# Weight sums of a seven-product matrix multiplication moved to accumulating DMAs in DRAM, with two of the seven split weights stored ahead and loaded as they are

## The chip, the cores and the metric

One NeuronCore of a Trainium2 chip runs one program. The metric is device microseconds (us) of one execution; less is better. Three runs of the kernel before took 936.91, 937.03 and 938.17 us, so its median is 937.03 us. Engines are named as the profile names them: PE (TensorE matmul; PEld its weight loads), DVE (VectorE), ACT (ScalarE), POOL (GpSimd) and SP (SyncE, which here only issues DMAs).

## What is computed

A decoder trunk of two layers on 512 tokens of width 1024, all float32: an mLSTM layer, then a gated linear attention (GLA) layer, each inside RMS norms with a residual. The change lies in the GLA layer, mostly in its last product:

```python
def gla_mixer(h, w_in, w_gate_up, b_gate, norm_w, w_out):
    p = jnp.einsum('btd,de->bte', _f32(h), _f32(w_in))      # q, k, v, z, r are slices of p
    ...
    o = gla_chunked(q * (G_KEY_HEAD ** -0.5), k, v, log_a)   # 4 heads, values 4 x 512
    on = o * lax.rsqrt(jnp.mean(o * o, axis=-1, keepdims=True) + NORM_EPS)
    y = on.reshape(B, T, D_INNER) * _f32(norm_w) * jax.nn.silu(z)
    return jnp.einsum('bte,ed->btd', y, _f32(w_out))         # (512 x 2048) by (2048 x 1024)
# in reference():  x = x + rms_norm(out, post_norm_w[i])
```

## The kernel before

**Split products.** PE multiplies in a reduced float format (fp32r). To keep float32 accuracy every operand is split in two: `hi` is the operand rounded (a CAST on ACT, line 137) and `lo` the remainder (a subtraction on DVE, line 138). Each product is three matmuls: hi by hi, hi by lo, lo by hi. Weights come from DRAM in chunks of 128 x 1024 (512 KB). A chunk is loaded into one of three `raw` buffers (SP, line 154) and split into one of four pairs of buffers `whi`, `wlo`; PE reads those. So a split of chunk number j+4 waits until PE is done with chunk j.

**Order.** PE, ACT and DVE run in the order in which the Python code emits the work. `run_jobs` goes through a list of jobs; ahead of each job it emits the splits of chunks up to `LA` = 3 chunks further on, then what earlier jobs deferred with `later(k, ...)` (k jobs later), then one item or more of `steps` and `spare`, and then the job itself. SP and POOL are ordered by the scheduler of the framework; each of them, too, works strictly in its order.

**The end of the GLA layer**, in the order of PE: for heads 0 to 3, v products (`gv`, 4 chunks a head), attention (`o`) and z products (`gz`, 4 chunks a head) alternate; the last of them is the attention of head 3, `g_att(3)`. Then comes the product by `w_out`. It is cut 2 x 2 x 2 and done with seven half-size products (Strassen-Winograd) instead of eight: P1 to P7, each of 4 chunks; a chunk meets 2 blocks of tokens, 12 matmuls in all. The seven need sums of the quarters A11, A12, A21, A22 of the weights: U = A21 + A22 for P5, U - A11 for P6, A12 - (U - A11) for P3, A22 - (U - A11) for P7. POOL forms them in SBUF, chunk by chunk (lines 1241, 1246, 1257, 1263). The other side needs sums of quarters of y: `combine` (lines 1200 to 1202), and one subtraction in `g_y` (line 1135), on POOL and DVE. Products go to PSUM in the order P1 and P5 in turn, P2 and P3 in turn, P6, the rest of P3, P7, P4. Each half row of the result is summed, squared for the norm (ACT, line 1304), multiplied by the norm's weights `pw` (POOL, line 1310; DVE for the last two), scaled and added to the residual `xr` (DVE, line 1326), and stored (SP, line 1327). The residual itself, `x1_d`, was written to DRAM at the start of the layer.

```python
        return source([(w_gout[1, 0, c], lambda: t5("sm")[:, 0:1024]), (w_gout[1, 1, c], None)], form=f,
                      after=to_s2, free=(1, 0))          # P5: loads A21 and A22, POOL adds them
    ...
    SRC = {"P1": p1, "P5": p5, "P2": p2, "P7": p7, "P3": lambda c: source([], form=lambda: raw12[c]),
           "P6": lambda c: source([], form=lambda: sm[c], free=(0, 0))}
```

Of the kernel before, what the change touches and what calls it, by code (L numbers as in the profile page):

```python
# [95 lines left out]
def tile_mlstm_gla(ctx, tc, xT, pvec, cst, wg, wgv, w_min, w_qk, w_v, w_mout,  # L96
# [8 lines left out]
    ctx.enter_context(tc.manual_schedule(engines={mybir.EngineType.PE, mybir.EngineType.Activation,  # L105
                                                  mybir.EngineType.DVE}))

# [949 lines left out]
    def full_qk(w, j, after):  # L1057
        def run(chunk):
            ev = gqk(w, j, chunk)
            later(1, lambda: (ev(), after and after()))  # L1060

        job(run, ring(w_gqk[w, j]))
# [16 lines left out]
    def gv_job(h, c):  # L1079
        def run(chunk):  # L1080
            if c == 0:
                st["gv", h] = [psum("gv") for _ in range(4)]
            pss = st["gv", h]
            natural(pss, chunk, 2 * c, ghi2, glo2, 8)
            if c == 3:
                def evac():
                    VS[h] = t2s("gvhi", 4, F32R), t2s("gvlo", 4, F32R)
                    for i in range(4):
                        hi, lo = VS[h][0][i], VS[h][1][i]
                        nc.scalar.activation(hi, pss[i], AF.Identity, scale=rcol[:, i:i + 1])  # L1090
# [5 lines left out]
        job(run, ring(w_gv[h, c]))  # L1096

# [31 lines left out]
    def g_y(h, vt):  # L1129
# [9 lines left out]
    def gz_job(n):  # L1139
        def run(chunk):  # L1140
# [10 lines left out]

        job(run, ring(w_gz[n]))

    job(lambda: nc.vector.reduce_max(mx, nref, axis=AX.X), n=0)
    gz_job(0)
# [9 lines left out]
    for h in range(NH):  # L1165
        if h + 1 < NH:
            for c in range(4):
                gv_job(h + 1, c)
        if h == NH - 1:
            job(lambda: [operand("2", k, Y[1, k]) for k in range(4)], n=0)  # L1170
            job(lambda: [combine(k, nc.gpsimd) for k in range(4)], n=0)
        job(lambda h=h: g_att(h))
        if h + 1 < NH:
            gz_job(4 * h + 4)
            job(lambda h=h: (g_rstd(h), split_scores(h + 1)), n=0)
            for i in range(1, 4):
                gz_job(4 * h + 4 + i)
# [17 lines left out]

    def combine(k, eng):

        y1, y2 = Y[0, k], Y[1, k]
        a, b = HALF
        eng.tensor_sub(y1[:, b], y2[:, b], y1[:, b])  # L1200
        eng.tensor_sub(y1[:, a], y1[:, b], y1[:, a])  # L1201
        eng.tensor_sub(y2[:, a], y2[:, a], y1[:, b])

# [5 lines left out]
    def block(name, k):  # L1209
        what, half = {"P1": ("1", 0), "P5": ("1", 1), "P2": ("2", 0), "P3": ("2", 1),  # L1210
                      "P7": ("3", 0), "P6": ("3", 1), "P4": ("4", k % 2)}[name]
        return [z[:, HALF[half]] for z in OPS[what, k // 2 if what == "4" else k]]

    bank, sums, parts = {}, {}, {}

    def product(name, to, chunks, tb, c0=0):
# [3 lines left out]
        for c, (whi, wlo) in enumerate(chunks):  # L1220
            for i in range(2):
# [8 lines left out]
    sm, raw11, raw12, raw22, last = ([None] * 4 for _ in range(5))  # L1230
    sub = nc.gpsimd.tensor_sub

    def p1(c):
        def f(a11):
            raw11[c] = a11
            return a11
        return source([(w_gout[0, 0, c], lambda: t5("a11")[:, 0:1024])], form=f, free=(0, 0))

    def p5(c):
        def f(a21, a22):  # L1240
            nc.gpsimd.tensor_add(a21, a21, a22)
            sm[c] = a21
            return a21

        def to_s2():
            sub(sm[c], sm[c], raw11[c])

        return source([(w_gout[1, 0, c], lambda: t5("sm")[:, 0:1024]), (w_gout[1, 1, c], None)], form=f,
                      after=to_s2, free=(1, 0))

    def p2(c):
        def f(a12):
            raw12[c] = a12
            return a12

        def to_s4():
            sub(raw12[c], raw12[c], sm[c])

        return source([(w_gout[0, 1, c], None)], form=f, after=to_s4, free=(0, 0))

    def p7(c):
        def f(a22):
            sub(sm[c], a22, sm[c])  # L1263
            raw22[c] = a22
            return sm[c]

        def to_p4():
            last[c] = split_chunk(raw22[c], "t2")

        return source([(w_gout[1, 1, c], None)], form=f, after=to_p4)  # L1270

    SRC = {"P1": p1, "P5": p5, "P2": p2, "P7": p7, "P3": lambda c: source([], form=lambda: raw12[c]),
           "P6": lambda c: source([], form=lambda: sm[c], free=(0, 0))}
    TO = {"P1": "a", "P6": "a", "P7": "a", "P4": "a", "P5": "c", "P3": "c", "P2": "d"}

    def prod_job(name, c, n=1, la=LA):
        def run(chunk):
            for tb in range(2):
                product(name, TO[name], [chunk], tb, c)
            if c == 3:  # L1280
                if name in ("P1", "P5", "P6", "P7"):
                    AFTER[name]()
                else:
                    later(8 if name == "P2" else 2, AFTER[name])

        job(run, SRC[name](c), n=n, la=la)

# [29 lines left out]

    def row_done(r):
# [13 lines left out]
    def after_p7():  # L1332
        for tb in range(2):
            out_part(2 + tb, 1, "a", "e5", tb)
        row_done(2)
        row_done(3)

    def after_p3():
        for tb in range(2):
            out_part(2 + tb, 0, "c", "u2", tb)  # L1340

    AFTER = {"P1": lambda: keep_copy("e1", "a"), "P5": lambda: keep_copy("e5", "c"), "P6": after_p6,
             "P2": lambda: [out_part(tb, 0, "d", "e1", tb) for tb in range(2)], "P7": after_p7, "P3": after_p3}

# [6 lines left out]
    for c in range(4):  # L1351
        prod_job("P1", c)
        prod_job("P5", c)
        if c == 1:
            job(lambda: (g_rstd(NH - 1), steps.extend(
                [lambda: tail_y(0), lambda: tail_y(2), lambda: None, lambda: None]
                + [lambda k=k: (combine(k, nc.vector), combine(k + 1, nc.vector)) for k in (4, 6)]
                + [lambda k=k: (operand("3", k, Y[0, k]), operand("3", k + 1, Y[0, k + 1])) for k in range(0, 8, 2)]
                + [lambda c=c: operand4(c) for c in range(4)])), n=0)

    def load_pw():
        st["pw"] = t5("pw")[:, 0:D]
# [97 lines left out]
```

## Time and profile before

| | |
|---|---|
| median of three runs | 937.03 us |
| the profiled execution: its time | 936.81 us |
| its span, first to last instruction | 935.1 us (1.7 us lie around it) |
| PE busy | 907.2 us, 97% of the span |
| DVE, ACT, POOL busy | 653.5, 523.2, 224.3 us |
[...]
| DMA, mean over the span | 117 GB/s |

The page cuts the span into 40 slices; the engines' digits there are tenths of busy time. A "wait" row says which instruction idled and what released it. The chain of waits follows the work that ended last back through what released it. A matmul's own duration in the records is longer than the step from one matmul to the next, since they are pipelined; the pace of PE is read from starts.

### The profile page before, as it was taken

The page shows a single profiled execution, that of the slowest core. Times are in us where ns is not written, and L with a number is a line of the kernel's source. Part 1 is how long each engine was busy: PE and PEld are TensorE (multiplying, and loading weights), DVE is VectorE, ACT ScalarE, POOL GpSimd, SP SyncE. Part 2 cuts the span into 40 slices and gives each one's busy share as a digit, 9 for nine tenths or more (in the row PEclk, how much of TensorE's full clock was granted, in tenths as well). Part 3 has the DMA queues.
Part 4 walks back from the last instruction along what each step waited for, and adds up shares of the span by engine and source line. Part 5 has one row for each costly group of instructions (what it writes and reads, how often), then busy time and mean ns, then how long its engine had stood idle before and what let it go on. Part 6 is the DMA issues. An engine that isn't in the chain of part 4 may idle for free. (4 is left out here: it accounts for less than half of the span.)

```text
span 935.1 us, 12315 instructions
## 1 busy us (share of the span) xinstructions
PE 907.2 (97%) x4624; PEld 761.7 (81%) x4624; DVE 653.5 (70%) x886; ACT 523.2 (56%) x876; POOL 224.3 (24%) x152
## 2 busy tenths in 40 slices
PE   9999999999999999999999999999999999978886
PEld 7887878878877888899999987778888888866665
DVE  5999897787795678787678666632445454598986
ACT  6856676655745657685666554553334342535653
POOL 0022563154230045332001100000001011275443
PEclk9999999999999999999999999999999999998999
DMA  8334353442431312323776322222222243230232
GB/s 308 123 108 146 113 174 119 146 137 97 151 113 46 121 64 86 124 103 115 222 229 226 131 73 85 68 68 94 90 67 91 68 158 113 91 112 23 68 123 102
DMA packets 40514, 109.82 MB, mean 117 GB/s; under 512 B 4416, under 2 KB 8896, under 8 KB 40448
## 3 DMA queue, kind: packets, MB, share of 16 engines
q1 hardware_dynamic: 40160, 108.75, 35.2%
q8 instruction: 38, 0.62, 0.3%
q10 hardware_dynamic: 288, 0.22, 0.1%
q14 instruction: 28, 0.23, 0.1%
HBM read 100.56 MB, written 8.39 MB: 117 GB/s over the span
## 5 line engine op out<-in xcount | busy, mean ns | idle before, releaser
L138 DVE TENSOR_TENSOR wlo<-raw,whi 128x1024 fp32r<-128x1024 f32 (+1 forms) x138 | 180.4, 1313 | 117.5 <-ACT whi L137 116.1
L137 ACT CAST whi<-raw 128x1024 fp32r<-128x1024 f32 (+1 forms) x138 | 142.6, 1038 | 96.4 <-PE gv L122 37.7
L381 POOL TENSOR_TENSOR vp<-V,wv 128x512 f32<-128x512 f32 x56 | 88.8, 1609 | 177.4 <-ACT V L469 109.5
L122 PE MATMUL op<-yhi,whi 128*128 128x256 f32 x256 | 73.4, 287 | 0.0
L122 PE MATMUL op<-yhi,wlo 128*128 128x256 f32 x256 | 72.5, 283 | 0.4 <-DVE wlo L138 0.4
L122 PE MATMUL op<-ylo,whi 128*128 128x256 f32 x256 | 72.8, 284 | 0.0
L384 DVE SCALAR_TENSOR_TENSOR vp<-V,wv 128x512 f32<-128x512 f32 x72 | 68.0, 987 | 0.0
L122 PE MATMUL gz<-g2h,whi 128*128 128x512 f32 x128 | 51.5, 403 | 0.4 <-PEq L1113 0.4
L122 PEld LDWEIGHTS op<-ylo,whi 128*128 128x128 f32 x256 | 49.1, 192 | 1.1 <-DVE ylo L138 0.6
L122 PE MATMUL gz<-g2h,wlo 128*128 128x512 f32 x128 | 49.9, 390 | 0.0
L122 PE MATMUL gz<-g2l,whi 128*128 128x512 f32 x128 | 49.8, 389 | 0.0
L122 PE MATMUL qk<-chi,whi 128*128 128x512 f32 x128 | 49.8, 389 | 0.0
L122 PE MATMUL qk<-chi,wlo 128*128 128x512 f32 x128 | 49.8, 389 | 0.0
L122 PE MATMUL qk<-clo,whi 128*128 128x512 f32 x128 | 49.8, 389 | 0.0
L122 PE MATMUL gv<-whi,g2h 128*128 128x512 f32 x128 | 49.8, 389 | 0.0
L122 PE MATMUL gv<-wlo,g2h 128*128 128x512 f32 x128 | 49.8, 389 | 0.0
L122 PE MATMUL gv<-whi,g2l 128*128 128x512 f32 x128 | 49.8, 389 | 0.0
L122 PEld LDWEIGHTS op<-yhi,wlo 128*128 128x128 f32 x256 | 49.1, 192 | 0.6 <-DVE wlo L138 0.6
L122 PEld LDWEIGHTS op<-yhi,whi 128*128 128x128 f32 x256 | 49.1, 192 | 0.5 <-issue 0.5
L122 PE MATMUL op<-whi,yhi 128*128 128x512 f32 x96 | 38.7, 403 | 8.9 <-ACT whi L137 8.9
L122 PE MATMUL op<-wlo,yhi 128*128 128x512 f32 x96 | 39.0, 406 | 8.6 <-DVE wlo L138 8.6
L686 POOL TENSOR_TENSOR sq<-sq 128x512 f32<-128x512 f32 x12 | 17.6, 1471 | 114.2 <-ACT sq L684 95.4
(283 smaller groups left out, 2582.0 us busy)
## 6 DMA issues: line engine op xcount, KB each, us to landing
raw<-in_w_min SPq DMA_DIRECT2D x30, 512.0 KB, 3.7
raw<-in_w_mout SPq DMA_DIRECT2D x29, 512.0 KB, 4.0
wv<-in_wgv SPq DMA_DIRECT2D x32, 256.0 KB, 3.6
raw<-in_w_qk SPq DMA_DIRECT2D x16, 512.0 KB, 3.6
raw<-in_w_gqk SPq DMA_DIRECT2D x16, 512.0 KB, 4.0
raw<-in_w_gz SPq DMA_DIRECT2D x16, 512.0 KB, 3.4
raw<-in_w_gv SPq DMA_DIRECT2D x16, 512.0 KB, 3.5
raw<-in_w_gout SPq DMA_DIRECT2D x12, 512.0 KB, 3.5
```

The costliest lines, as they stand in the source:

```text
L122: nc.tensor.matmul(out, lhsT=lhsT, rhs=rhs, start=start, stop=stop, skip_group_check=more)
L137: nc.scalar.copy(hi, src)
L138: nc.vector.tensor_sub(lo, src, hi.bitcast(F32))
L381: nc.gpsimd.tensor_mul(j, V[h][i], w)
L384: nc.vector.scalar_tensor_tensor(j, V[h][i], 1.0, w, op0=ALU.mult, op1=ALU.mult, accum_out=o)
L686: nc.gpsimd.tensor_add(sqs[0], sqs[0], sqs[vt])
```

## The change

Four parts.

1. **Sums in DRAM.** The four kinds of sums (U, W, Z, R; 4 chunks each) become DRAM tensors. Signs are moved to the other side, so that only additions are left: U = A21 + A22, W = A11 + U, Z = A12 + W, R = A11 + A21. The weights in `w_gout` are unchanged; parts of y and the second half of `pw` change sign instead. Each sum is a copy (DRAM to DRAM) and then an accumulating DMA on it, 32 DMAs of 512 KB, issued by POOL beside the q and k products of the GLA layer. POOL does no arithmetic on weights any more.
2. **P3 and P7 split ahead.** Eight extra jobs (`pre_job`) between the z and v jobs load a chunk of Z or R, split it (ACT, DVE) and store both halves to DRAM (SP, four stores). At P3 and P7 POOL's DMAs load the halves straight into `whi` and `wlo`.
3. **y side and results on DVE.** `combine` for all eight k, the subtraction in `g_y` and the multiplications by `pw` move from POOL to DVE. For token rows 2 and 3 the scaled result is added to `x1_d` by an accumulating DMA (POOL) and `x1_d` is copied to the output (SP, DRAM to DRAM); rows 0 and 1 are as before.
4. **Order.** One more chunk of look-ahead at `g_att(3)` and at the jobs beside the extra ones; P4's chunks become jobs of their own, loaded again from `w_gout`; deferred steps are spaced differently; POOL's order is now the code's.

```diff
-HLA = 3
+HLA = 6
+PRE = ("P3", "P7")
     def split_chunk(raw, kind):
+        if kind == "pre":
+            hi = wp.tile([P, 1024], F32R, tag="whi", bufs=4, name="whi")
+            lo = wp.tile([P, 1024], F32R, tag="wlo", bufs=4, name="wlo")
+            for to, of in zip((hi, lo), raw):
+                nc.gpsimd.dma_start(to, of)
+            return [hi[:, 0:T], hi[:, T:]], [lo[:, 0:T], lo[:, T:]]
...
+    def weights(what, c):
+        return {"P1": w_gout[0, 0, c], "P2": w_gout[0, 1, c], "P4": w_gout[1, 1, c], "P5": wsum["U", c],
+                "P6": wsum["W", c], "P3": wsum["Z", c], "P7": wsum["R", c]}[what]
+    def pre_job(name, c):
+        def run(chunk):
+            for to, of in zip(wpre[name, c], chunk):
+                for i in range(2):
+                    nc.sync.dma_start(to[:, i * T:(i + 1) * T], of[i].bitcast(F32))
+        job(run, source([(weights(name, c), None)], "t2"), n=0)
+    def wsum_start(n, c):
+        nc.gpsimd.dma_start(wsum[n, c], {"U": w_gout[1, 0, c], "W": w_gout[0, 0, c], "Z": w_gout[0, 1, c],
+                                       "R": w_gout[0, 0, c]}[n])
+    def wsum_add(n, c):
+        nc.gpsimd.dma_start(wsum[n, c], {"U": w_gout[1, 1, c], "W": wsum["U", c], "Z": wsum["W", c],
+                                         "R": w_gout[1, 0, c]}[n], accum_op=ALU.add,
+                            max_dma_last_dim=4096)
...
-            nc.gpsimd.tensor_sub(y[:, HALF[1]], y[:, HALF[1]], y[:, HALF[0]])
+            nc.vector.tensor_sub(y[:, HALF[1]], y[:, HALF[0]], y[:, HALF[1]])
...
-            job(lambda: [combine(k, nc.gpsimd) for k in range(4)], n=0)
-        job(lambda h=h: g_att(h))
+        job(lambda h=h: g_att(h), la=LA + (h == NH - 1))
...
-            nc.gpsimd.tensor_add(a21, a21, a22)
-            sub(sm[c], sm[c], raw11[c])
-            sub(raw12[c], raw12[c], sm[c])
-            sub(sm[c], a22, sm[c])
...
+    def row_added(r):
+        c = row_rstd(r)
+        for m in (0, 1):
+            o, sl = parts[r, m], slice(m * T, (m + 1) * T)
+            nc.vector.scalar_tensor_tensor(o, o, c, st["pw"][:, sl], op0=ALU.mult, op1=ALU.mult)
+            nc.gpsimd.dma_start(x1_d[r, :, sl], o, accum_op=ALU.add)
+        nc.sync.dma_start(out[r * P:(r + 1) * P, :], x1_d[r])
...
-    job(lambda: product("P4", "a", last, 0), n=2)
+    for c in range(4):
+        def run(chunk, c=c):
+            last[c] = chunk
+            product("P4", "a", [chunk], 0, c)
+        job(run, chunk_of("P4", c, True), n=2)
```

Three places show what moves. First, POOL from the last attention on. Before:

```order
L1241 TENSOR_TENSOR sm<-sm,raw 128x1024
L1246 TENSOR_TENSOR sm<-sm,a_8332 128x1024
L1246 TENSOR_TENSOR sm<-sm,a_8423 128x1024
L1246 TENSOR_TENSOR sm<-sm,a_8621 128x1024
L1257 TENSOR_TENSOR raw<-raw,sm 128x1024 x4
L1263 TENSOR_TENSOR sm<-raw,sm 128x1024 x4
L1310 TENSOR_TENSOR o<-o,pw 128x512 x6
```

In the changed kernel POOL's order ends like this (`wpP` are the stored halves):

```order
L163 DMA whi<-wpP_253 128x1024
L163 DMA wlo<-wpP_254 128x1024
L163 DMA whi<-wpP_255 128x1024
L163 DMA wlo<-wpP_256 128x1024
L163 DMA whi<-wpP_257 128x1024
L163 DMA wlo<-wpP_258 128x1024
L163 DMA whi<-wpP_259 128x1024
L163 DMA wlo<-wpP_260 128x1024
L1341 DMA x_d<-o 128x512 x4
```

No arithmetic of POOL is left there: sixteen loads of halves and four accumulating stores.

Second, SP at the z products of head 1 (`gz`, the four loads after eight of `gv`). Before:

```order
L154 DMA raw<-in_w_gv 128x1024 x3
L154 DMA raw<-in_w_gz 128x1024 x4
L154 DMA raw<-in_w_gv 128x1024 x4
L154 DMA raw<-in_w_gz 128x1024 x4
L154 DMA raw<-in_w_gv 128x1024 x3
```

Now:

```order
L155 DMA raw<-in_w_gv 128x1024 x3
L155 DMA raw<-in_w_gz 128x1024
L155 DMA raw<-wsZ_269 128x1024
L155 DMA raw<-in_w_gz 128x1024
L1051 DMA wpP_245<-khi_7515 128x512
L155 DMA raw<-wsZ_270 128x1024
L155 DMA raw<-in_w_gz 128x1024
L1051 DMA wpP_245<-khi_7516 128x512
```

The first load of a sum, Z of chunk 0, stands ahead of the second of these `gz` loads, and the stores stand between loads.

Third, DVE at the end of the program, from the results of P7 on (`klo` is the split of P4's weights). Before:

```order
L138 TENSOR_TENSOR klo_9120<-raw,khi_9118 128x512
L138 TENSOR_TENSOR klo_9121<-raw,khi_9119 128x512
L1314 TENSOR_TENSOR o<-op,e_8782 128x512
L1314 TENSOR_TENSOR o<-op,e_8784 128x512
L1314 TENSOR_TENSOR o<-op,u_9086 128x512
L1314 TENSOR_TENSOR o<-op,u_9088 128x512
L1314 TENSOR_TENSOR o<-op,e_8802 128x512
L1314 TENSOR_TENSOR o<-op,e_8804 128x512
```

Now:

```order
L1324 TENSOR_TENSOR o<-op,e_8964 128x512
L1324 TENSOR_TENSOR o<-op,e_8966 128x512
L1330 TENSOR_TENSOR rso<-ssq 128x1
L1340 SCALAR_TENSOR_TENSOR o<-o,rso,pw 128x512 x2
L139 TENSOR_TENSOR klo_9371<-w_9223,khi_9369 128x512
L139 TENSOR_TENSOR klo_9372<-w_9223,khi_9370 128x512
L1330 TENSOR_TENSOR rso<-ssq 128x1
L1340 SCALAR_TENSOR_TENSOR o<-o,rso,pw 128x512 x2
```

The split of P4's last chunk now stands behind the whole of row 2's result, which waits for the end of P7.

## Rows read from the trace of the kernel before

**Rows 1.** The page: busy time of each engine, and PE in 40 slices.

```profile
PE 907.2 (97%) x4624; PEld 761.7 (81%) x4624; DVE 653.5 (70%) x886; ACT 523.2 (56%) x876; POOL 224.3 (24%) x152
PE   9999999999999999999999999999999999978886
```

**Rows 2.** Windows (start:end, length, busy us and count by engine, clock, DMA share, GB/s).

```profile
0.00:827.80 827.80, 825.06 (x4287) 698.45 (x4288) 562.86 (x788) 473.21 (x789) 174.34 (x127) 1.00 0.37 121
827.80:928.50 100.70, 82.11 (x338) 63.28 (x336) 88.02 (x95) 48.75 (x84) 49.94 (x25) 0.97 0.24 81
841.50:844.50 3.00, 0.99 (x2) 0.48 (x3) 2.16 (x3) 3.00 (x4) 0.17 (x1) 0.50 0.00 0
640.00:820.00 180.00, 180.00 (x833) 150.44 (x832) 85.44 (x94) 76.00 (x92) 19.16 (x14) 1.00 0.29 97
0.00:23.00 23.00, 21.03 (x79) 16.11 (x80) 13.49 (x22) 14.73 (x22) 0.20 (x4) 1.00 0.86 307
```

**Rows 3.** Waits of PE over the whole span (us in total, times, longest).

```profile
PE op L122 <- DVE wlo L138: 9.0, 10, 1.5
PE op L122 <- ACT whi L137: 8.9, 2, 7.1
```

**Rows 4.** Chain of waits, pieces in order of time (start, us, what).

```profile
779.78 9.97 PE gv L122 x44
...
917.30 11.19 PE op L122 x48
928.51 0.70 ACT sq L1304 x2
...
930.71 1.30 DVEq L1456
```

**Rows 5.** Timeline of PE (start, us, instruction, idle before it and its releaser).

```profile
693.06 0.44 PE L122 MATMUL gz<-g2h,whi 128*128 128x512 f32 x1
...
699.02 0.79 PE L122 MATMUL gz<-g2h,whi 128*128 128x512 f32 x1
...
827.52 0.44 PE L122 MATMUL op<-whi,yhi 128*128 128x512 f32 x1
...
843.05 0.80 PE L122 MATMUL op<-whi,yhi 128*128 128x512 f32 x1 [7.14 <-ACT whi L137]
```

**Rows 6.** Timeline of DVE in the seven products.

```profile
843.03 1.23 DVE L138 TENSOR_TENSOR wlo<-sm,whi 128x1024 fp32r<-128x1024 f32 x1 [0.24 <-ACT whi L137]
...
845.30 3.41 DVE L138 TENSOR_TENSOR wlo<-sm,whi 128x1024 fp32r<-128x1024 f32 x1
...
918.13 0.16 DVE L1321 TENSOR_TENSOR rso<-ssq 128x1 f32<-128x1 f32 x1 [0.29 <-ACT sq L1304]
...
924.89 0.75 DVE L1326 SCALAR_TENSOR_TENSOR o<-o,rso,xr 128x512 f32<-128x512 f32 x1 [0.60 <-ACT rso L1323]
```

**Rows 7.** Timeline of POOL.

```profile
522.21 1.29 POOL L297 TENSOR_TENSOR sq<-sq 128x512 f32<-128x512 f32 x1 [2.16 <-ACT sq L294]
...
573.08 0.63 POOL L1021 TENSOR_SCALAR_AFFINE_SELECT GA<-GA 128x128 f32<-128x128 f32 x2 [0.46 <-ACT GA L1019]
...
844.33 3.30 POOL L1246 TENSOR_TENSOR sm<-sm,a 128x1024 f32<-128x1024 f32 x1 [6.13 <-DVE wlo L138]
```

**Rows 8.** Groups of DVE by form, 640 to 780 us (count, busy, mean ns, idle).

```profile
L138 DVE TENSOR_TENSOR wlo<-raw,whi 128x1024 fp32r<-128x1024 f32 x23 | 28.2, 1226 | 47.7 <-ACT whi L137 47.7
L1132 DVE TENSOR_TENSOR pt<-pt,rs 128x512 f32<-128x512 f32 x8 | 5.3, 685 | 0.0
```

**Rows 9.** Groups of DVE and of ACT by form, 640 to 930 us.

```profile
L138 DVE TENSOR_TENSOR ylo<-pt,yhi 128x512 fp32r<-128x512 f32 x24 | 27.9, 1203 | 1.4 <-ACT yhi L137 1.2
L1202 DVE TENSOR_TENSOR pt<-pt,pt 128x256 f32<-128x256 f32 x4 | 1.7, 417 | 0.0
L137 ACT CAST whi<-raw 128x1024 fp32r<-128x1024 f32 x34 | 35.6, 1050 | 51.0 <-PE gv L122 37.7 <-issue 8.6 <-DMA raw<-in_w_gout 3.6
```

**Rows 10.** Timeline of SP: its loads of `gz` for head 1, and one load.

```profile
655.39 16.61 SPq L154 DMA_DIRECT2D raw<-in_w_gz  x4
...
750.00 0.42 SPq L195 DMA_DIRECT2D sm<-in_w_gout  x1
```

**Rows 11.** DMA issues over the span (count, KB each, median us from issue to landing).

```profile
raw<-in_w_gz SPq DMA_DIRECT2D x16, 512.0 KB, 3.4
x_d<-xn SPq DMA_DIRECT2D x8, 256.0 KB, 2.6
xr<-x_d SPq DMA_DIRECT2D x8, 256.0 KB, 4.1
out_dram<-o SPq DMA_DIRECT2D x8, 256.0 KB, 2.1
```

More of the change, by code (lines that the diff above doesn't have):

```diff
@@ L105, in tile_mlstm_gla @@
     ctx.enter_context(tc.manual_schedule(engines={mybir.EngineType.PE, mybir.EngineType.Activation,
-                                                  mybir.EngineType.DVE}))
+                                                  mybir.EngineType.DVE, mybir.EngineType.Pool}))
     def t2(name, dt=F32):
@@ L157, in split_chunk @@
     def split_chunk(raw, kind):
+        if kind == "pre":
[4 more added lines that the diff above has]
+            return [hi[:, 0:T], hi[:, T:]], [lo[:, 0:T], lo[:, T:]]
+        if kind == "pre2":
+            hi, lo = t2s("khi", 2, F32R), t2s("klo", 2, F32R)
+            for to, of in zip((hi, lo), raw):
+                for i in range(2):
+                    nc.gpsimd.dma_start(to[i], of[:, i * T:(i + 1) * T])
+            return hi, lo
         if kind == "ring":
@@ L1024, in tile_mlstm_gla @@
     kept = {}
+    def weights(what, c):
+        return {"P1": w_gout[0, 0, c], "P2": w_gout[0, 1, c], "P4": w_gout[1, 1, c], "P5": wsum["U", c],
+                "P6": wsum["W", c], "P3": wsum["Z", c], "P7": wsum["R", c]}[what]
+    wpre = {(n, c): [dp.tile([P, 1024], F32, name=f"wp{n}{c}{i}") for i in range(2)]
+            for n in PRE for c in range(4)}
+    def pre_job(name, c):
+        def run(chunk):
+            for to, of in zip(wpre[name, c], chunk):
+                for i in range(2):
+                    nc.sync.dma_start(to[:, i * T:(i + 1) * T], of[i].bitcast(F32))
+        job(run, source([(weights(name, c), None)], "t2"), n=0)
+    wsum = {(n, c): dp.tile([P, 1024], F32, name=f"ws{n}{c}") for n in "UWZR" for c in range(4)}
+    def wsum_start(n, c):
[5 more added lines that the diff above has]
+                            max_dma_last_dim=4096)
     def kept_a(w, j, kind, la=LA):
@@ L1060, in run @@
             later(1, lambda: (ev(), after and after()))
-        job(run, ring(w_gqk[w, j]))
+        job(run, ring(w_gqk[w, j]), b=3)
+    job(lambda: spare.extend([lambda n=n, c=c: wsum_start(n, c) for n in "URWZ" for c in range(4)]
+                             + [lambda n=n, c=c: wsum_add(n, c) for n in "URWZ" for c in range(4)]), n=0)
     rest = [(w, j) for h in range(NH) for w, j in ((0, 2 * h), (1, 2 * h), (0, 2 * h + 1), (1, 2 * h + 1))
@@ L1094, in run @@
                 later(1, evac)
-        job(run, ring(w_gv[h, c]))
+        job(run, ring(w_gv[h, c]), b=1)
     mx = cp.tile([P, 1], F32, name="mx")
@@ L1150, in run @@
             later(1, act)
-        job(run, ring(w_gz[n]))
+        job(run, ring(w_gz[n]), la=la)
+    pre = [lambda n=n, c=c: pre_job(n, c) for n in PRE for c in range(4)]
     job(lambda: nc.vector.reduce_max(mx, nref, axis=AX.X), n=0)
@@ L1167, in tile_mlstm_gla @@
             for c in range(4):
+                if c == 2 and h and pre:
+                    pre.pop(0)()
                 gv_job(h + 1, c)
@@ L1194, in operand, with combine @@
         split(*OPS[name, k], src)
-    def combine(k, eng):
+    def combine(k):
         y1, y2 = Y[0, k], Y[1, k]
         a, b = HALF
-        eng.tensor_sub(y1[:, b], y2[:, b], y1[:, b])
-        eng.tensor_sub(y1[:, a], y1[:, b], y1[:, a])
-        eng.tensor_sub(y2[:, a], y2[:, a], y1[:, b])
+        for to, x, y in ((y1[:, b], y1[:, b], y2[:, b]), (y1[:, a], y1[:, b], y1[:, a]),
+                         (y2[:, a], y1[:, b], y2[:, a])):
+            nc.vector.scalar_tensor_tensor(to, x, -1.0, y, op0=ALU.mult, op1=ALU.subtract)
     def operand4(c):
@@ L1212, in block, with chunk_of @@
         return [z[:, HALF[half]] for z in OPS[what, k // 2 if what == "4" else k]]
+    def chunk_of(name, c, last=False):
+        if name in PRE:
+            return source([], "pre2" if last else "pre", form=lambda: wpre[name, c], free=(0, 0))
+        if last:
+            return source([(weights(name, c), lambda: t5("w4")[:, 0:1024])], "t2", free=(0, 0))
+        return ring(weights(name, c))
     bank, sums, parts = {}, {}, {}
@@ L1227, in product @@
                 mm(ps, yl, whi[i], False, k == 7, more)
[L1230 to L1240, printed above, removed]
-            nc.gpsimd.tensor_add(a21, a21, a22)
-            sm[c] = a21
-            return a21
-        def to_s2():
-            sub(sm[c], sm[c], raw11[c])
[L1248 to L1256, printed above, removed]
-            sub(raw12[c], raw12[c], sm[c])
-        return source([(w_gout[0, 1, c], None)], form=f, after=to_s4, free=(0, 0))
-    def p7(c):
-        def f(a22):
-            sub(sm[c], a22, sm[c])
[L1264 to L1273, printed above, removed]
+    last = [None] * 4
     TO = {"P1": "a", "P6": "a", "P7": "a", "P4": "a", "P5": "c", "P3": "c", "P2": "d"}
@@ L1280, in run @@
             if c == 3:
[L1281 to L1286, printed above, removed]
+                AFTER[name]()
+        job(run, chunk_of(name, c), n=n, la=la)
     def keep_copy(name, to):
@@ L1334, in after_p7, with after_p2 @@
             out_part(2 + tb, 1, "a", "e5", tb)
-        row_done(2)
-        row_done(3)
+            later(1 + tb, lambda tb=tb: row_added(2 + tb))
     def after_p3():
         for tb in range(2):
-            out_part(2 + tb, 0, "c", "u2", tb)
+            later(1 + tb, lambda tb=tb: out_part(2 + tb, 0, "c", "u2", tb))
+    def after_p2():
+        for tb in range(2):
+            later(3 + tb, lambda tb=tb: (out_part(tb, 0, "d", "e1", tb), part_scale(tb, 0, parts[tb, 0])))
     AFTER = {"P1": lambda: keep_copy("e1", "a"), "P5": lambda: keep_copy("e5", "c"), "P6": after_p6,
-             "P2": lambda: [out_part(tb, 0, "d", "e1", tb) for tb in range(2)], "P7": after_p7, "P3": after_p3}
+             "P2": after_p2, "P7": after_p7, "P3": after_p3}
     def tail_y(v):
@@ L1353, in tile_mlstm_gla @@
         prod_job("P5", c)
+        if c == 0:
+            job(lambda: steps.extend([lambda k=k: (combine(k), combine(k + 1)) for k in (0, 2)]), n=0)
         if c == 1:
@@ L1356, in tile_mlstm_gla @@
                 [lambda: tail_y(0), lambda: tail_y(2), lambda: None, lambda: None]
-                + [lambda k=k: (combine(k, nc.vector), combine(k + 1, nc.vector)) for k in (4, 6)]
+                + [lambda k=k: (combine(k), combine(k + 1)) for k in (4, 6)]
                 + [lambda k=k: (operand("3", k, Y[0, k]), operand("3", k + 1, Y[0, k + 1])) for k in range(0, 8, 2)]
@@ L1368, in tile_mlstm_gla @@
         prod_job(name, c)
-    job(lambda: [load_res(r) for r in (2, 3)], n=0)
     prod_job("P7", 3)
```

21 lines of the change are left out of this document (13 added, 8 removed).

## The prediction

> **What bounds the kernel now.** I read the busy shares first: PE is busy 97% of the span, and only the last tenths of its row fall under 9 [rows 1]. So I cut the span where the seven products begin. Until then PE misses 2.7 us of 827.8, and no change to other engines' work can win more there; in the products, 827.8 to 928.5 us, it is busy 82.1 of 100.7 us; the last 6.6 us have no matmul [rows 2]. The waits name the releasers: 8.9 us for a `whi` on ACT, one wait alone being 7.1 us, and 9.0 us in ten waits for a `wlo` on DVE [rows 3]. These are splits of weight chunks. [...]
>
> How much is there to win? Where nothing is late PE needs 9.97/44 = 0.2266 us a matmul [rows 4]. The products are 7 x 4 x 12 = 336 matmuls: 76.1 us. One norm's matmul in between costs about 0.5 us (the 5.96 us between the starts of two neighbouring z jobs, less 24 x 0.2266) [rows 5]. They begin at 827.5 [rows 5] and could end at 904.1; they end at 928.5. **24.4 us are lost**, 18.6 to waits and the rest to the low clock.
>
> Why are the splits late? DVE is busy 88.0 of those 100.7 us, POOL 49.9 [rows 2]. A chunk's `wlo` takes 1.23 us when POOL is quiet, and 3.41 us when it starts at 845.30 inside a POOL addition that runs from 844.33 to 847.63 [rows 6, 7]: DVE ends about 1.1 us after POOL does. The same form of `wlo` takes 1.226 us on average at 640 to 780 us, where POOL does little; a 512-wide operation takes 0.685 us there, but `ylo` averages 1.203 us at 640 to 930 [rows 8, 9]. So POOL's arithmetic both forms the sums late and holds DVE up.
>
> **What the change does to this, part by part.**
>
> *POOL's arithmetic.* All 16 weight sums of 1024 columns, 12 quarter sums and 6 scalings leave POOL in the products. DVE gets 12 quarter sums and two scalings more and loses the 8 splits of P3 and P7. Counting its new order from the last attention's results on: 13 `wlo` x 1.23, 37 operations of 512 x 0.69, 12 scalar_tensor_tensor of 512 x 0.75, 32 of 256 x 0.42, 4 small ones x 0.16 [rows 6, 8, 9] = 16.0 + 25.5 + 9.0 + 13.4 + 0.6 = 64.5 us, against 77 us that PE needs. ACT loses eight casts of 1.05 us [rows 9] and was at 48.7 [rows 2]. Neither is the bound any more. PE's big wait (P5, chunk 1) goes twice over: with `ylo` at 0.69 us DVE is through its backlog some 9 us earlier, and the added look-ahead puts that split ahead of the last attention's results. [...] What is late next is a transfer, below.
>
> *Splits moved ahead.* Eight chunks cost 1.05 us on ACT and 1.23 on DVE each, between 640 and 820 us, where DVE is busy 85 and ACT 76 of 180 us [rows 2]: hidden, since a split runs two 5.4 us jobs ahead of PE. If that cover were gone it would be up to 18 us in all. SP issues 32 stores and 8 loads more at 0.42 us [rows 10], 17 us in 180; loads queue behind a store that waits for its split, some us of the 30 that loads are ahead (worked out under the rivals). The eight subtractions of `g_y` cost DVE 8 x 0.42 us: hidden likewise.
>
> *Sums.* 32 DMAs of 512 KB, from the last addition of POOL at 523.5 us [rows 7] on, beside loads that move about 100 GB/s. I cost them nothing; that is the third rival's place.
>
> *Loading the halves.* A pair (`whi`, `wlo`, 1.05 MB) may start when PE has left the chunk four before, and is needed three chunks, 36 x 0.2266 = 8.2 us, later. POOL issued no DMA before, so its price is bounded by rows of other queues: 3.4 us if both land as one 512 KB load does, 6.8 us one after the other [rows 11], and at the far end 16.4 us, as four 256 KB loads of what a DMA had written, 4.1 us each [rows 11]. I take 6.8, as these are 512 KB loads. P3's first three stand alone: no wait. The last of P3 and P7's four come in a row: PE takes 2.72 us a pair, a DMA at the best rate on record, 307 GB/s [rows 2], 3.42; by the fifth that is 2.8 us, 9.6 against 8.2. **Term: 1 us**, ends 0 and 41 (five pairs late by 8.2 us). [...] No row here shows a DMA of POOL.
>
> *P4.* Its last chunk's split now stands behind row 2's result on DVE and ACT. From the end of P7: two additions 1.4, the square's end about 0.3, then 0.16 + 0.60 for the norm factor, two scalings 1.5, the split's first half 0.7 [rows 6, 8]: 4.7 us, and 5.4 for the second. PE asks for the first after 19 matmuls, 4.3 us, and for the second 0.7 us later. **Term: 1 us**, ends 0 and 2.
>
> *The end.* Row 1's last chain is as before: 6.6 us from the last matmul [rows 2, 4]. Rows 2 and 3 take an accumulating store, then a copy. Row 3's value is there about 8 us after P7, 4 us before PE ends; the store lies between 2.6 us (a plain one) and 6.7 (a load and a store in turn: 4.1 + 2.6), the copy between 2.1 and 6.2 [rows 11]; at the middles, 4.7 + 4.2, it ends 1.7 us before row 1's store. **Term: 0**, ends 0 and 2.
>
> Sum: 904.1 + 1 + 1 + 6.6 = 912.7 us of span, and 1.7 us around it: 914.4. The profiled execution's 936.81 us is 0.2 under the median of 937.03, so against that median: **about 915 us**, 2.4% less. The floor, with both terms 0, is 912.4.
>
> **The rivals.**
>
> *B, halves land late* (faster, by less). POOL's DMAs may cost more than SP's. If a pair takes 11 us instead of 8.2, each of P3's first three waits 2.8 us, and in the row of five the first and the fifth: 14 us, so about 929. For: no row shows this queue, and PE asks for 385 GB/s in P7 where 307 is the best on record. Against: 8.2 us is more than twice one landing. [...]
>
> *C, the sums are late* (**slower**). SP works in order, and its load of Z, chunk 0, now stands between two z loads. It would come to it at about 661 us (655.39 plus a third of 16.6) [rows 10]. The z job behind it starts on PE at 699.0 [rows 5] and needs 3.4 + 1.05 + 1.23 = 5.7 us from issue to split: so Z may arrive until 693 with no loss. Z of chunk 0 is the 13th accumulation, and the first can't start before POOL has passed a selection at about 574 [rows 7]. Run one by one, they may take 119/13 = 9.2 us each; above (119 + 22)/13 = 10.8 us the change is slower than before. Bounds from rows: 1.7 us each at 307 GB/s, and 12.0 us if two reads and two half writes follow one another (3.4 + 3.4 + 2 x 2.6) [rows 2, 11]; at 12 us Z comes at 730 and the time is about 951. Against: up to eight can be in flight, and DMA is busy about a third there [rows 2].
>
> *D, the wait only changes its name* (no gain). DVE's order has 24 quarter sums between the splits of P1, P5 and P2; if each chunk from P5 on waited 1.2 us for them, PE would lose the same 20 us. Against: 64.5 us of work in 77.
>
> **How the numbers follow.** Forecast 0.65: 912 to 919. B 0.19: 919 to 933. C 0.08 over 937, and 0.02 more for other losses (a buffer that comes free late in the z jobs). D 0.06: 932 to 939. Range 911.5 to 930: it leaves out the far part of B, all of C and D: about 0.19. About 0.2%, 1.9 us, is what a measurement of this kernel can tell from no change. Faster by more than that: 0.65 + 0.19 + 0.03 of D = 0.87; within it 0.03; slower 0.10.
>
> **What would show it.** Right: PE's slices at 9 to the end; no wait of PE for ACT over 1 us after the last attention; `wlo` at 1.23 us and `ylo` at 0.69 throughout the products; clock 1.0; P4's wait near 1 us. B: PE waiting for `whi` from POOL's DMAs in P3 and P7. C: a gap in PE near 699 us, SP waiting for `wsZ`. D: PE waiting for DVE in P1 to P2. My reading fails if DVE's operations stay long with POOL's arithmetic gone, or if the last copy of `x1_d` ends the span.

## The result, and the profile after

The changed kernel takes **917.0 us** (median of four runs, 915.08 to 917.5) against 937.37 us for the kernel before in the same comparison: a ratio of 0.9778, with a 95% interval of 0.9761 to 0.9795. The forecast was 915 us, the range 911.5 to 930. The profiled execution has a span of 915.8 us, 1.7 us under its own time of 917.5 us, as it was before.

The page of the changed kernel, busy times and PE in 40 slices, as [rows 1]:

```profile
PE 902.4 (99%) x4624; PEld 760.7 (83%) x4624; DVE 630.6 (69%) x916; ACT 523.3 (57%) x885; POOL 183.2 (20%) x162
PE   9999999999999999999999999999999999999995
```

PE has as many matmuls as before and is now busy to the last slice; POOL lost 41 us of work. The windows of the changed kernel (start:end, length, then busy us and count of PE, PEld, DVE, ACT and POOL, clock, DMA share, GB/s), as [rows 2]:

```profile
0.00:827.50 827.50, 824.30 (x4282) 697.14 (x4283) 571.38 (x818) 481.55 (x807) 171.12 (x142) 1.00 0.50 157
827.50:910.00 82.50, 78.15 (x345) 63.60 (x343) 59.25 (x99) 41.75 (x79) 12.09 (x20) 0.99 0.66 204
```

Until the products nothing changed for PE: 3.2 us are missing instead of 2.7. In the products DVE's work fell from 88.0 to 59.3 us, POOL's from 49.9 to 12.1, and the clock is 0.99 instead of 0.97 (1.00 from 841.5 to 844.5 us, where it was 0.50 behind PE's wait of 7.1 us [rows 2, 5]). What PE still waits for, over the whole span (us in total, times, longest; to be held against the 9.0 and 8.9 us of [rows 3]):

```profile
PE warm L123 <- DVE warm L289: 1.6, 1, 1.6
PE op L123 <- DMA wlo<-wpP: 0.6, 1, 0.6
PE gz L123 <- PEq L1156: 0.5, 1, 0.5
PE op L123 <- DVE wlo L139: 0.4, 1, 0.4
```

Only the second line lies in the products. The groups of DVE from 828 us on (count, busy us, mean ns, idle), as [rows 6, 8, 9]:

```profile
L139 DVE TENSOR_TENSOR wlo<-raw,whi 128x1024 fp32r<-128x1024 f32 x13 | 15.8, 1220 | 3.2 <-ACT whi L138 3.2
L139 DVE TENSOR_TENSOR ylo<-pt,yhi 128x512 fp32r<-128x512 f32 x13 | 8.3, 685 | 0.2
L1251 DVE SCALAR_TENSOR_TENSOR pt<-pt,pt 128x256 f32<-128x256 f32 x16 | 6.3, 418 | 0.0
```

`wlo` takes 1.22 us and `ylo` 0.69, as they do where POOL is still; before, `ylo` averaged 1.20 [rows 9]. The chain of waits at its end (start, us, what), as [rows 4]:

```profile
878.88 8.16 DMA wlo<-wpP
887.04 0.04 issue
887.08 19.21 PE op L123 x83
...
906.32 0.70 ACT sq L1314 x2
...
908.51 1.30 DVEq L1487
```

PE's last matmul ends at 906.3 us, 22 us earlier than before. But behind it come 9.5 us instead of 6.6. The copies and stores of the end, SP's timeline and the DMA issues from 890 us on (count, KB each, median us to landing; before, the stores landed in 2.1 us [rows 11]):

```profile
905.07 0.60 SPq L1342 DMA_DIRECT2D out_dram<-x_d  x1
905.76 1.00 SPq L1349 DMA_DIRECT2D out_dram<-o  x2
907.75 0.50 SPq L1342 DMA_DIRECT2D out_dram<-x_d  x1
909.17 0.99 SPq L1349 DMA_DIRECT2D out_dram<-o  x2
```

```profile
x_d<-o POOLq DMA_DIRECT2D x4, 256.0 KB, 5.1
out_dram<-x_d SPq DMA_DIRECT2D x2, 512.0 KB, 5.9
out_dram<-o SPq DMA_DIRECT2D x4, 256.0 KB, 5.5
```

Row 3's copy is issued at 907.75 us and lands 5.8 us later; row 1's last two stores stand behind it on SP's queue from 909.17 and take 5.0 us each (row 0's two, issued at 905.76, take 5.9).

### The profile page after: what moved, and what is told of

It reads as the page before. It is cut to its first block, busy times and chain, and to the rows that moved or that the text cites. A ratio compares the mean times of both kernels' runs of the same rounds, so it can differ in the third digit from the quotient of the medians.

```text
span 915.8 us, 12449 instructions
## 1 busy us (share of the span) xinstructions
PE 902.4 (99%) x4624; PEld 760.7 (83%) x4624; DVE 630.6 (69%) x916; ACT 523.3 (57%) x885; POOL 183.2 (20%) x162
## 5 line engine op out<-in xcount | busy, mean ns | idle before, releaser
L139 DVE TENSOR_TENSOR wlo<-raw,whi 128x1024 fp32r<-128x1024 f32 (+1 forms) x146 | 186.3, 1284 | 98.8 <-ACT whi L138 98.1
L138 ACT CAST whi<-raw 128x1024 fp32r<-128x1024 f32 (+1 forms) x146 | 149.9, 1036 | 79.0 <-PE gv L123 24.2
L163 POOL DMA_DIRECT2D whi<-wpP x8 | 4.3, 536 | 244.7 <-DMA raw<-in_w_gout 216.9
L123 PE MATMUL gz<-g2h,wlo 128*128 128x512 f32 x128 | 49.9, 390 | 0.0
L123 PE MATMUL z<-hhi,whi 128*128 128x512 f32 x112 | 44.1, 394 | 0.0
L123 PE MATMUL z<-hlo,whi 128*128 128x512 f32 x112 | 43.7, 390 | 0.0
```

Of the source, the lines that this page charges most:

```text
L123: nc.tensor.matmul(out, lhsT=lhsT, rhs=rhs, start=start, stop=stop, skip_group_check=more)
L138: nc.scalar.copy(hi, src)
L139: nc.vector.tensor_sub(lo, src, hi.bitcast(F32))
L163: nc.gpsimd.dma_start(to, of)
```

## Experiments

Three questions were open: which part of the change brings the 20 us, and by what mechanism; whether the end can be mended; and what the sums cost when they come late.

### Which part: the sums on POOL left out, or the splits ahead undone

`b_nosum` takes the kernel before and leaves only the sums out:

```diff
-            nc.gpsimd.tensor_add(a21, a21, a22)
...
-            sub(sm[c], sm[c], raw11[c])
...
-            sub(raw12[c], raw12[c], sm[c])
...
-            sub(sm[c], a22, sm[c])
```

> The kernel before, with its 16 weight sums of 1024 columns on POOL left out: P5, P6, P3 and P7 multiply by weights that are not summed; all else is as before, with the splits in the products and the quarter sums on POOL. Theory: with the sums neither late nor in DVE's way the 7.1 us wait and most waits for wlo go: 917 to 925 us. Rival (DVE's own work, eight splits more than after the change, is the bound): PE still waits 10 us or more for DVE: 930 us or more.

Measured: 917.44 us (916.31 to 918.15), ratio to before 0.9794 [0.9779, 0.9809]. That is the time of the changed kernel, with every split still in the products and the quarter sums still on POOL. So **leaving out the 16 weight sums on POOL is enough for the whole 20 us**, and the theory held. The rest of the change has two further effects, which cancel. From the first to the last matmul of the products `b_nosum` takes 81.6 us (826.4 to 908.0) and the changed kernel 78.3 (828.0 to 906.3), but behind the last matmul `b_nosum` has 6.6 us and the changed kernel 9.5. With a better end (`end_direct3`, 913.97 us, below) the changed kernel is 3.5 us faster than `b_nosum`, and the intervals don't touch. No run moves only the quarter sums or only the scalings, so what those bring by themselves is not shown.

`no_pre` takes the changed kernel and undoes the splits ahead:

```diff
-PRE = ("P3", "P7")
+PRE = ()
```

> The changed kernel without the splits ahead: P3 and P7 load their summed weights and split them in the products, as P6 does; the sums stay DMAs. Theory (POOL's arithmetic was what made the splits late): DVE gets 8 x 1.22 = 9.8 us back on its 59 and ACT 8.4 on its 42, both still under PE's 77; PE waits at most 4 us: 916 to 921 us. Rival (it is the splits ahead that free DVE): PE waits for wlo again, 9 us or more: 926 us or more.

Measured: 918.06 us, ratio 0.98 [0.9785, 0.9815], 1.1 us over the changed kernel, which the two intervals don't separate. The trace shows what the splits ahead saved. Groups of DVE from 828 us on, and PE's waits from 800 us on:

```profile
L139 DVE TENSOR_TENSOR wlo<-raw,whi 128x1024 fp32r<-128x1024 f32 x20 | 24.3, 1222 | 3.9 <-ACT whi L138 3.9
```

```profile
PE op L123 <- DVE o L1324: 0.9, 1, 0.9
PE op L123 <- ACT u L1301: 0.7, 1, 0.7
```

Seven splits more fall behind 828 us, each as short as ever, and PE waits 1.6 us in the products instead of 0.6. DVE had the room for them. With the better end of `end_direct3` the same edit was run again:

> As end_direct3, without the splits ahead of P3 and P7. Theory (the splits ahead are worth about 1 us as long as POOL is still, as 918.06 against 917.0 says): 1 us over end_direct3, 915 to 916 us. Rival (they are worth nothing, the 1 us lies in the different ends): the same time as end_direct3 or less.

Measured: 916.09 us (0.9775 [0.9762, 0.9788]) against 913.97 for `end_direct3` (0.9748 [0.9734, 0.9761]), so here the splits ahead are worth 2.1 us, twice what the theory had; its sign holds.

### By what: POOL's running, or the late sum

`b_idle` keeps POOL busy in the kernel before, but nothing waits for what it makes. At each of the four places of `b_nosum`, the line reads like this:

```diff
-            sub(sm[c], sm[c], raw11[c])
+            [nc.gpsimd.tensor_add(idle, idle, sm[c][:, i * 256:(i + 1) * 256]) for i in range(4)]
```

> The kernel before, with each of the 16 weight sums on POOL replaced by four additions of 256 columns that read the same chunk at the same place and go into a tile that nothing reads; P5, P6, P3 and P7 multiply by weights that are not summed. POOL is as busy as before, and no split waits for it. Theory (it is POOL's running that makes DVE late): wlo and ylo are long again, DVE is busy 80 us or more in the products, and the time is 928 to 940 us. Rival (it is the wait for a late sum): 917 to 921 us, as with the sums left out.

Measured: 930.16 us (929.09 to 930.93), 0.9927 [0.9912, 0.9942]. Groups of DVE from 828 us on, first of `b_idle`, then of `b_nosum`:

```profile
L138 DVE TENSOR_TENSOR ylo<-pt,yhi 128x512 fp32r<-128x512 f32 x17 | 17.3, 1065 | 0.1
L138 DVE TENSOR_TENSOR wlo<-sm,whi 128x1024 fp32r<-128x1024 f32 x11 | 15.2, 1384 | 4.1 <-ACT whi L137 4.1
L138 DVE TENSOR_TENSOR wlo<-a,whi 128x1024 fp32r<-128x1024 f32 x2 | 3.5, 1752 | 0.0
```

```profile
L138 DVE TENSOR_TENSOR ylo<-pt,yhi 128x512 fp32r<-128x512 f32 x14 | 10.1, 762 | 0.2
L138 DVE TENSOR_TENSOR wlo<-sm,whi 128x1024 fp32r<-128x1024 f32 x11 | 13.4, 1220 | 5.5 <-ACT whi L137 5.5
L138 DVE TENSOR_TENSOR wlo<-a,whi 128x1024 fp32r<-128x1024 f32 x2 | 2.4, 1218 | 0.0
```

POOL's running alone costs 930.2 - 917.4 = **12.7 us**. I put what is left to the kernel before, 937.1 - 930.2 = **6.9 us**, down to the sums that come late; that is not shown (see below). The windows of `b_idle` (828 to 932 us, and its first part) and of `b_nosum` show the way:

```profile
828.00:932.00 104.00, 81.31 (x336) 64.03 (x334) 79.74 (x97) 49.09 (x86) 61.36 (x51) 0.92 0.22 76
828.00:850.00 22.00, 16.22 (x56) 11.95 (x55) 16.81 (x16) 8.86 (x12) 21.02 (x20) 0.77 0.13 48
```

```profile
828.00:932.00 104.00, 77.82 (x332) 63.01 (x330) 64.46 (x94) 49.48 (x86) 10.12 (x9) 0.95 0.22 75
```

51 us more of POOL make DVE 15.3 us busier with the same work. PE then waits 5.1 us at 840 us for a `whi` that stands on ACT behind squares of the last attention's results, which wait for DVE; the clock falls to 0.77 in the stretch from 828 to 850 us. Two cautions. POOL is 11.6 us busier here than in the kernel before, and row 3's scalings stand behind the additions on POOL, so 3 of the 12.7 us lie behind the last matmul (928.0 - 918.4 = 9.6 us instead of 6.6). And the additions of 256 columns hold DVE less than the sums that they stand for. The kernel before in the same window:

```profile
828.00:932.00 104.00, 81.91 (x337) 63.09 (x335) 90.48 (x99) 49.74 (x88) 49.74 (x25) 0.97 0.25 84
```

Against `b_nosum` DVE is 26.0 us busier there with 39.6 us more of POOL, 0.66 us for each; in `b_idle` 15.3 with 51.2, 0.30 for each. So some or all of the 6.9 us can be the same hold. The 7.1 us wait at 843 us was not for a late sum either: POOL's last sum for P5 ended at 838.2 us, and the cast that PE waited for stood on ACT until 841.96, behind the last of those squares, as in `b_idle`.

`pool_busy` puts such additions into the changed kernel:

```diff
...
+            if name in ("P1", "P5", "P2", "P6"):
+                [nc.gpsimd.tensor_add(idle, idle, chunk[0][i // 2][:, i % 2 * 256:i % 2 * 256 + 256].bitcast(F32))
+                 for i in range(4)]
             for tb in range(2):
                 product(name, TO[name], [chunk], tb, c)
```

> The changed kernel with arithmetic put back on POOL that nothing waits for: for each of the 16 chunks of P1, P5, P2 and P6, as soon as its whi is there, four additions of 256 columns into a tile that is never read, some 50 us of POOL in all. Theory (an operation of POOL holds up DVE's): wlo goes from 1.22 us on average to 1.8 or more, DVE's busy time in the products from 59 to 72 us or more, PE waits for splits again for 3 to 12 us: 920 to 930 us. Rival (only that the sums came late counted): wlo stays at 1.22 us and the time at 917.

Measured: 941.39 us (940.09 to 942.32), 1.0047 [1.0032, 1.0063]: all the gain is lost, and more than the 3 to 12 us that I gave it. Its groups of DVE from 828 us on, and its windows:

```profile
L139 DVE TENSOR_TENSOR wlo<-raw,whi 128x1024 fp32r<-128x1024 f32 x13 | 19.6, 1511 | 2.6 <-ACT whi L138 2.6
L1251 DVE SCALAR_TENSOR_TENSOR pt<-pt,pt 128x256 f32<-128x256 f32 x16 | 13.4, 864 | 0.0
```

```profile
850.00:870.00 20.00, 16.12 (x47) 11.59 (x48) 18.32 (x19) 7.78 (x12) 15.76 (x18) 0.74 0.44 157
```

A 256-wide operation takes 864 ns instead of 418, DVE is busy 83.2 us by 930, over PE's 77. Here POOL also issues the loads of halves, and they stand behind its additions. Of PE's waits from 800 us on, 8.3 us are for a `wlo` on DVE and 2.2 for a half; no run separates DVE's delay from that of the halves further.

Two more kernels were meant to separate them. In both the additions came out otherwise than their text says: 1024 columns wide, one a chunk, in a tile that takes one of the seven wide buffers, and reading no chunk. So POOL ran ahead with them. `pool_p1p5` is the changed kernel with

```diff
+    idle = [t5("idle")[:, 0:1024]]
...
+            if name in ("P1", "P5"):
+                nc.gpsimd.tensor_add(idle[0], idle[0], idle[0])
```

and `no_pre_busy` is `no_pre` with the same line for P1, P5, P2 and P6.

> As pool_busy, but the four additions on POOL stand only at the 8 chunks of P1 and P5: 20 of them, some 20 us of POOL, fall behind 828 us, and no load of a half stands behind them. Full dose: 51 us of POOL made DVE busy 83.2 instead of 59.3 us, 0.47 us per us. Theory (DVE's total against PE's 77 us decides): DVE about 59.3 + 9.4 = 69 us, under 77, PE waits 2 us at most: 917 to 919 us. Rival (what counts is the tight place behind the last attention, 840 to 862 us, where DVE has a backlog): PE waits 4 us or more there: 921 us or more.

Measured: 921.7 us, 0.9823 [0.9808, 0.9838]. Seven of the eight additions ran at 746 to 762 us, where PE then waits 1.4 us that the changed kernel doesn't have; the eighth fell behind the first two loads of halves. Timelines of POOL and of DVE at that place:

```profile
850.79 1.93 POOL L1294 TENSOR_TENSOR idle<-idle 128x1024 f32<-128x1024 f32 x1
```

```profile
849.38 1.23 DVE L139 TENSOR_TENSOR wlo<-raw,whi 128x1024 fp32r<-128x1024 f32 x1 [0.26 <-ACT whi L138]
850.52 3.36 DVE L1175 TENSOR_TENSOR pt<-pt,rs 128x512 f32<-128x512 f32 x2
853.97 1.29 DVE L139 TENSOR_TENSOR ylo<-pt,yhi 128x512 fp32r<-128x512 f32 x2
```

By chance this is the cleanest look at the mechanism: **one** addition of 1.93 us, and a pair of DVE operations that takes 1.29 us elsewhere takes 3.36, 2.07 more. All of it falls on the first of the two: 2.76 us instead of 0.68. PE, which had no wait there, waits 0.79 and 0.76 us at 855.5 and 856.8, and its clock is 0.91 from 850 to 870 us. DVE's total in 828 to 932 is 62.1 us, far under 77; so here DVE's total does not decide, and the tight place behind the last attention does. On the dose that it was meant to test the run says nothing. The first operation of the pair ends 0.56 us after the addition does, nearly its whole own length of 0.68, so by these times it stood still while the addition ran and was not merely slowed. By the records it had begun 0.27 us ahead of the addition, and yet it was the one that stood.

> As pool_busy (941.4 us), without the splits ahead: POOL has the same 64 additions and no DMA of halves between them; DVE has seven or eight splits more in the products. Theory (DVE is the bound once POOL runs): DVE goes from 83 to about 93 us, the products get longer by about as much: 946 to 953 us. Rival (what made pool_busy slow is the loads of halves that stood behind POOL's additions): without them 925 to 935 us.

Measured: 919.96 us, 0.981 [0.9795, 0.9825]. All 16 additions ran at 746.7 to 784.6 us, before the products. So it says nothing on its question, but gives a control: 38 us of POOL where DVE has room cost 1.9 us over `no_pre`, which the two intervals don't separate; PE's waits show 1.2 of it (`gv` for a `wlo`).

### The end, and a faster kernel

`end_direct` accumulates the values of rows 2 and 3 straight into the output, which x1 has been copied into long before:

```diff
-            nc.gpsimd.dma_start(x1_d[r, :, sl], o, accum_op=ALU.add)
-        nc.sync.dma_start(out[r * P:(r + 1) * P, :], x1_d[r])
+            nc.gpsimd.dma_start(out[r * P:(r + 1) * P, sl], o, accum_op=ALU.add)
```

and, ahead of the loop over the `w_gqk` chunks of `rest`:

```diff
+    job(lambda: [nc.sync.dma_start(out[r * P:(r + 1) * P, :], x1_d[r]) for r in (2, 3)], n=0)
```

> The changed kernel, except that x1 of rows 2 and 3 is copied into the output long before the products, and their last values are accumulated straight into the output: the two 512 KB copies at the end are gone. Theory (the copies stand ahead of row 1's last two stores on SP's queue and slow them to 5.5 us): these land in about 2.1 us, as before the change, the part behind the last matmul goes from 9.5 to about 6.6 us, the span from 915.8 to about 913 and the time from 917.0 to about 914. Rival (POOL's accumulating stores are what takes the DMA then): the last stores keep 5 us and the time stays at 917.

Measured: 915.0 us (913.98 to 916.52), 0.9761 [0.9748, 0.9775]. Its interval overlaps that of the changed kernel. The end is as said: last matmul at 908.1, span 914.7, 6.6 us. But PE waits 1.4 us more ahead of the products. I put that to SP's early copies and moved them, in `end_direct2` to POOL (`nc.gpsimd` for `nc.sync`), behind the job of its last selection, `gscore(NH - 1)`, in `end_direct3` further on, behind `job(branch)`:

> As end_direct, but the two early copies of x1 into the output are issued by POOL behind the last selection (about 631 us), when all sums have been issued, instead of by SP at about 440 us, where loads stood behind them. Theory (those copies cost PE its waits between 520 and 640 us, 1.4 us more than in the changed kernel): the waits go, the end stays at 6.6 us, the products start near 828.0 as in the changed kernel, span near 912.8, time 913 to 914.5. Rival (the later start in end_direct was chance): the time stays at 915.

> As end_direct2, with POOL's two copies of x1 into the output behind the program's one branch (about 637 us) instead of ahead of it. Theory (PE's 3.8 us wait behind the branch in end_direct2 came from the copies that held the DMA engines just then, where the code behind the branch has to be fetched): that wait is back at about 0.5 us, nothing else waits, the end stays at 6.6 us: span 912.5 to 913.5, time 914 to 915. Rival (an accumulating store into the output or the copy costs PE somewhere else): 917 us or more.

Measured: 919.1 us (0.9809 [0.9796, 0.9823]) and **913.97 us** (0.9748 [0.9734, 0.9761]), 3.0 us under the changed kernel (the intervals just touch) and the fastest of all. Row 1's last two stores land in 2.1 us (row 0's two in 4.6), with POOL's accumulating stores still there, so it was not these that slowed row 1's stores. `end_direct2` lost 2 us instead of gaining 3. PE's waits, in it and in `end_direct3`:

```profile
PE gz L123 <- DVEq L1156: 3.8, 1, 3.8
```

```profile
PE gsc L123 <- DVE sqk L1022: 0.8, 1, 0.8
PE gz L123 <- PEq L1156: 0.3, 1, 0.3
```

L1156 is the program's one branch. With the copies ahead of it in POOL's order PE stands 3.8 us behind it, with the same copies behind it in that order 0.3. The theory on `end_direct`'s early waits fell: `gsc` waits 0.8 us in `end_direct3` too, where SP issues no such copy.

### The sums late

The Z sums go behind the last selection and behind N copies that nothing reads:

```diff
...
+    extra = [dp.tile([P, 1024], F32, name=f"ex{i}") for i in range(4)]
+    job(lambda: [nc.gpsimd.dma_start(extra[i % 4], w_gout[0, 0, i % 4]) for i in range(12)]
+        + [wsum_add("Z", c) for c in range(4)], n=0)
```

> The changed kernel with the four Z sums issued later: behind POOL's last selection, at about 631 us, and behind 12 more copies of 512 KB from DRAM to DRAM that nothing reads. At the 3.3 us a DMA of the 32 in the changed kernel (523.6 to about 629 us) Z of chunk 0 is ready at about 631 + 13 x 3.3 = 674 us. Theory (SP's loads have a cover until 693 us): SP waits for wsZ from 661 us on, but PE loses nothing: 917 us. Rival (loads behind it are late at once): PE waits near 699 us, 920 us or more.

> As late12 with 32 such copies. Theory: Z of chunk 0 is ready at about 631 + 33 x 3.3 = 740 us, 47 us after the cover ends at 693; SP stands still and every later load with it: PE waits near 699 us for a weight chunk, 40 to 50 us in all: 957 to 967 us. Rival (copies alone run at 1.7 us each, the best rate in the trace of before): ready at 687 us, no loss, 917 us.

Measured: 921.13 us (0.9833 [0.9818, 0.9848]) and 935.96 us (0.9989 [0.9979, 0.9998]). Copies alone went faster than I had it: in `late32` POOL issued one every 1.8 us, and the Z sums from 686.2 us on, so Z was ready at 695 and not at 740. In `late12` the sums were out at 649 to 652 us, SP came to Z at 667.17 and PE lost nothing near 699; it lost 2.2 us more than the changed kernel behind the branch at 636 us, where the copies were running. That is nearly all that the trace can show, since the two profiled spans lie only 2.4 us apart (918.2 and 915.8); the rest of the 4.1 us between the medians stays open. So the theory's mechanism held, and its 917 us did not. In `late32` SP stood at Z until 695.3, 2.3 us past the 693 that the prediction had as the end of the cover. The chain of waits there:

```profile
686.18 9.08 DMA wsZ<-wsW
...
695.32 0.33 SPq L155
...
695.74 10.20 DMA raw<-in_w_gz
...
706.03 1.05 ACT whi L138
...
707.11 1.20 DVE wlo L139
```

```profile
PE gz L123 <- DVE gvlo L1134: 11.5, 1, 11.5
PE gz L123 <- PEq L1156: 2.9, 1, 2.9
```

(the second fence: PE's waits). The z load behind Z took 10.2 us, not the 3.4 of [rows 11], beside the three sums that still ran. So being 2.3 us past the cover cost 11.5 at that place, and the run is 19 us longer in all, 2.4 of them at the branch as in `late12`; PE's clock was 0.95 from 700 to 827.5 us, where the changed kernel has 1.00. Rival C's mechanism is real, and dearer than one for one.

## Why the prediction was right, point by point

- **The bound and the floor.** The last matmul was put at 904.1 + 1 + 1 = 906.1 us and ended at 906.3. The products began 0.5 us later than taken (828.0 instead of 827.5); the two terms of 1 us came to 0.6 and 0; about 1 us lies in no wait that the trace names. PE's starts place some of it: 1.1 us for the norm's matmuls at 839 us, where the sum had 0.7, and 0.3 us beside the wait for the half.
- **POOL's arithmetic.** Right, by experiment: leaving out 16 sums gives all of it. Of that, 12.7 us come back with POOL's running alone (some 3 of them at the end of that run); whether the other 6.9 are late sums or a longer hold of DVE is open. The prediction had the big wait of P5 gone twice over; `b_nosum`, with the weight sums gone but without the added look-ahead, keeps 1.4 us of it, and the changed kernel none. `wlo` at 1.22 and `ylo` at 0.69 came as forecast. DVE's sum of 64.5 us was 58.8 from 828 us on: some of its work lay before.
- **Splits ahead.** That they are hidden was right: PE is busy 180.0 of the 180 us from 640 to 820. The prediction did not ask what they bring; it is 1 to 2 us. Its reasoning, DVE under 77 us, holds with them in the products too.
- **Sums at no cost.** Right: SP came to Z at 661.31 us, 661 was the forecast, and the Z sums had been issued by 619.3. The eight DMAs in flight that spoke against rival C are there: POOL issues eight copies from 523.63 to 527.7 us without a wait and the ninth at 529.77, when the first has landed. The cover to 693 us is bounded only loosely: SP passed Z at 667.2 us in `late12` without a wait of PE near 699, and at 695.3 in `late32` with one. The price past the cover was not right: the 3.4 us for a load is the median of the kernel before [rows 11]; beside three sums that still ran it took 10.2.
- **Loading the halves.** Term 1 us, measured 0.6 us, one wait in P7. The working had the fifth pair of the row late; it was the third, and the two behind it landed in at most 8.0 us without a wait, so the lag did not grow from pair to pair as taken. A half lands in 4.1 (`whi`) and 6.0 us (`wlo`, issued second), medians, and the one that PE waited for in 8.16: just at the 8.2 us window. A pair that takes 11 us, rival B's, did not show: the slowest half landed in 8.2, and POOL issued each in 0.5 to 0.6 us with DVE at work beside it.
- **P4.** Term 1 us, measured 0: PE shows no wait, one weight load 0.19 us.
- **The end: the step that failed.** "Row 1's last chain is as before: 6.6 us ... Term: 0". It is 9.5 us. I asked only whether row 3's copy ends before row 1's store does, and not what stands behind it: the stores of row 1 are issued on the same queue 1.4 us after the copy and land in 5.0 us instead of 2.1. `end_direct` and `end_direct3` take the copy away and have 6.6 and 6.7 us. Whether the shared queue does it or the DMA engines' work on the copy, no run tells apart. With 9.5 us in its place the sum is 915.6 us of span; 915.8 was measured.

The end's term was bounded by 0 and 2 us and so was missed by 0.9 us beyond its bounds. The two smaller terms erred the other way, by 1.4 us together, and the late start took 0.5; the 917 us stayed within 2 us of the forecast because the large terms, floor and waits, were sized from rows, and, by luck, because the small misses partly cancelled.

## What to carry to other kernels

Arithmetic on POOL is not free work on an idle engine: it can stop DVE, here for 0.3 to 1.1 us for each us that it runs, so what counts is whether DVE has room in that very stretch, not over the span. Sums of weights can go to accumulating DMAs long before they are needed, and then cost little (here the products began 0.5 us later); but count what each DMA delays behind it, on its queue or on the DMA engines, at the end of a program (here 5.0 us for a store instead of 2.1) and around a branch (2.7 to 3.8 us of PE instead of 0.3 to 0.5) above all.

## What the runs showed that I had not expected

- **A branch and copies.** PE's wait behind the one branch is 0.3 to 0.5 us where POOL has no copies just ahead of it (before, changed kernel, `end_direct3`) and 2.7, 2.9 and 3.8 us where copies from DRAM to DRAM stand there (`late12`, `late32`, `end_direct2`). The branch instruction on PE's weight-load queue takes 3.4 us before and 3.8 in the changed kernel, and while it runs one packet of 16 KB (0.02 MB) starts on an instruction queue in each. The instruction queues carry ten packets between 600 and 655 us in these two, in `late12` and in `end_direct2`. So there is a fetch at that place; that the copies delay it is argued, not shown: how long it took beside them, no row shows.
- **A store behind a copy.** Row 1's two stores of 256 KB landed in 5.0 us each behind a 512 KB copy from DRAM to DRAM, and in 2.1 us without it in `end_direct3`.
- **The size of POOL's hold.** 12.7 and 24.4 us by additions whose result nobody reads; 2.07 us of DVE by a single one of 1.93 us.
